# Six products of the second matmul taken to a second level inside PSUM, in the first two superblocks of an MLP block

## The chip, the cores and the metric

The kernel runs on one core of one Trainium2 chip. The metric is the device time in microseconds, the median of several runs. TensorE does the matmuls, VectorE sums, ScalarE copies and applies gelu, GpSimd casts, sums and issues DMAs, and SyncE issues most DMAs. "us" is a microsecond throughout.

## The reference

`x` is 8 x 1024 x 1024, `w1` 1024 x 4096 and `w2` 4096 x 1024, all float32. What is computed:

```
h = x @ w1
h = 0.5 * h * (1 + np.tanh(np.sqrt(2 / np.pi) * (h + 0.044715 * h ** 3)))
return (h @ w2).astype(np.float32)
```

## The kernel before

The 8192 rows of `x` are worked off in eight superblocks of 1024 rows. Each superblock has a first matmul (x by w1, with gelu, giving the four blocks g11, g12, g21, g22) and a second one (g by w2). Operands are float16, sums in PSUM float32.

**Seven products for eight.** Each matmul is cut into 2 x 2 blocks, and seven products of sums of blocks stand for the eight plain block products (Winograd's form of Strassen). The numbers 1, 2, 3, 4, 5, 6, 7 name the products; `W_SUM` says how the operand of the w side is summed for 5, 6, 7 and 4, and `S_SUM` how the other side is summed for 7, 6, 5 and 3. The same scheme can be applied again inside a product, with half the rows, half the columns and half the contraction: seven steps in place of eight, on matmuls of 256 columns. That is the second level. It needs inner sums of both operands.

**Which superblocks have it.** From superblock 2 on, both matmuls work on the second level (`Pair` and `Inner`, L659 and L984), with inner sums of w1 and w2 that lie in DRAM (`w1_d` with keys "s1" to "s5", `in_d`). Superblocks 0 and 1 build these sums and mostly work on one level: `matmul1` (L519) and `matmul2_made` (L807). In `matmul2_made` a product has four row groups q of 128 rows, each with 16 matmuls of 512 columns into one PSUM bank (`matmuls2`, L1057). The products run in the order 1, 2, 5, 6, 3, 7, 4.

**What sets the order.** Each engine's queue is in order. What VectorE does beside the products stands in the table `FILL` (L44): one row of jobs behind each (product, row group). `gmq` makes the g-side sums of product m; `wmq` makes the w2 sum m for one quarter of the contraction; `pmn` makes inner sum n of w2's product m and has GpSimd store it to `in_d`; `xm` sums blocks of the next superblock's x; `qm` sums w1 for the next superblock; `im` makes inner sums of x or of w1. In superblock 1 the w2 sums made by `make` (L839) are also stored to DRAM. `post` (L882) copies or adds a finished bank and issues the output store. SyncE's queue holds the loads of w2 (`bring`, L813, with float32 pieces that are cast in superblock 0), stores of the raw float16 blocks (`keep`, L832), the transposing loads of the next x, and loads of w1 (`MadeQuad`, L186), in the order of the program. SBUF tiles come from pools of fixed size: "u" has 26 buffers, "gc" 4, "tmp" 10; PSUM has 8 banks. A new tile waits until the last reader of the one it replaces has finished, which can be a DMA.

**Lines that the prediction's rows name.** L135 is the helper `tt` for VectorE sums, L159 `load_in_order` on SyncE, L162 the ScalarE copy, L165 the GpSimd cast, L195 loads of w1, L306 inner sums on GpSimd in later superblocks, L353 matmuls on zeros at the start, L485 one-level matmuls of the first matmul, L504 differences of g, L1012 second-level sums of g in later superblocks, L1059 one-level matmuls of the second matmul.

Of the kernel before, what the change touches and what calls it, by code (L numbers as in the profile page):

```python
# [39 lines left out]
def slots(table):  # L40
    return {(int(k[0]), int(k[1])): v.split() for k, v in (row.split(":") for row in table.split(";"))}


FILL = (  # L44
    slots("""10:g60 p15;11:g61 p16;12:g62 p17;13:g63
    ;20:g50 w50 w51;21:g51 w52;22:w53 g52;23:g53 p14
    ;50:w60 w61;51:w62 w63;52:g30 g31;53:g32 g33
    ;60:w70 w71;61:w72 w73;62:w40 w41;63:w42 w43
    ;73:x5;40:x7 x6;41:x3 q5;42:q6 q7 q4
    ;43:i2 i3 i1 i5""".replace("\n    ", "")),  # L50
    slots("""10:g60 w50;11:g61 w51;12:g62 w52;13:g63 w53
    ;20:g50 p55;21:g51 p56;22:g52 p57;23:g53 p54
    ;50:w60 w61;51:w62 w63;52:g30 g31;53:g32 g33
    ;60:p65 w70;61:p66 w71;62:p67 w72;63:p64 w73
    ;30:w40 w41;31:w42 w43;32:p75;33:p76
    ;70:p77 p74;71:x5 p45;72:x7 p46;73:x6 p47
    ;40:p44;41:x3;42:i2;43:i3""".replace("\n    ", "")),
)


# [11 lines left out]
def kernel(  # L72
# [113 lines left out]
    class MadeQuad:  # L186
# [52 lines left out]
            if self.store:  # L239
                nc.gpsimd.dma_start(out=w1_at(self.q, m), in_=halves(self.ops[m]))  # L240

        def inner_sums(self, m):
            t = self.ops[m].rearrange("p (h k c) (e n) -> p h k c e n", h=2, k=2, e=2)
            s = up.tile([P, 2, 4, 2, P], DT, name="u")

            def operand(b):
                if isinstance(b, int):
                    return s[:, :, list(S_SUM).index(b)]
                return t[:, :, int(b[1]) - 1, :, int(b[0]) - 1, :]

            for j, (u, op, v) in S_SUM.items():
                tt(operand(j), operand(u), operand(v), op, True)
            nc.gpsimd.dma_start(
                out=w1_at(self.q, f"s{m}"),
                in_=s.rearrange("p h j c n -> p h (j c n)"),
            )
# [55 lines left out]
    class XOps(dict):  # L312
# [5 lines left out]
            for m, b in S_TERM.items():  # L318
                self[m] = blocks[b]

        def make(self, m, cols=slice(None), pin=False):
            u, op, v = {5: ("21", ADD, "22"), 7: ("11", SUB, "21"), 6: ("22", SUB, 7), 3: ("12", SUB, 6)}[m]
            if m not in self:
                self[m] = self.blocks["21"] if m == 7 else unit(KH, HT)
            in0, in1 = (self[b] if isinstance(b, int) else self.blocks[b] for b in (u, v))
            tt(self[m][:, :, cols], in0[:, :, cols], in1[:, :, cols], op, pin)

        def make_inner(self, m):
# [187 lines left out]
            t = g[b][:, c:c + KH, :].rearrange("p c n -> p (c n)")  # L516
            yield t.rearrange("p (e n) -> p e n", e=2)

    def matmul1(xs, sb, quads, start=None):  # L519
        g = g_tiles()  # L520

        def gelu(b, c, src):
            gelu_into(g[b][:, c, :], src)
# [22 lines left out]
        for j in range(NI // 2):  # L546
# [62 lines left out]
            if end:  # L609
                six(0)  # L610
                gelu("11", cs[0], a[0])
                six(1)
                gelu("11", cs[1], a[1])
                for h in range(2):
                    five(h)
                for h in range(2):
                    seven(h)
                    gelu("22", cs[h], p5[h])
                    three(h)
                for h in range(2):  # L620
                    product(banks_a[h], source, xs, 4, cs[h], False)
                    gelu("21", cs[h], banks_a[h])
                for h in range(2):
                    add(t[h], banks_c[h])
                    gelu("12", cs[h], t[h])
            else:
                first = j == 0
                five(0)
                if not first:
                    gelu("11", cs[0], a[0])  # L630
                five(1)
                six(0)
                if not first:
                    gelu("11", cs[1], a[1])
                six(1)
                for h in range(2 if first else 0):
                    gelu("11", cs[h], a[h])
                three(0)
                three(1)
                seven(0)  # L640
                seven(1)
                for h in range(2):
                    gelu("22", cs[h], p5[h])
                for h in range(2):
                    add(t[h], banks_c[h])
                late = (source, cs, banks_a, t)
            for job in jobs[half:]:
                job()
            if sb == 1 and j < 2 * len(SPLIT_IN_M1):
                splits = split_in_m1(SPLIT_IN_M1[j // 2], j % 2)  # L650
            if sb == 1 and j > 4:
# [152 lines left out]
        rows = out2[r0:r0 + HT // 2, o0:o0 + OH].rearrange("(i p) n -> p i n", p=P)  # L804
        return nc.gpsimd.dma_start(out=rows, in_=src, **kw)  # L805

    def matmul2_made(sb, g, keep_w1, xb):  # L807


        raw = {b: [] for b in BLOCKS}  # L810
# [25 lines left out]

        over = {6: "11", 7: "12", 4: "21"}

        def make(m, q):  # L839
            if m not in sums:  # L840
                sums[m] = raw[over[m]] if m in over else [unit(2, HALF) for _ in range(NI // QC)]
            u, op, v = W_SUM[m]
            in0, in1 = (sums[b][q] if isinstance(b, int) else raw[b][q] for b in (u, v))
            tt(sums[m][q], in0, in1, op, True)
            if sb:
                n = 1 if q < 2 else 2
                nc.gpsimd.dma_start(out=w2_at(q, m)[:, :n], in_=sums[m][q][:, :n])

# [3 lines left out]
        def rows(t, q):  # L852
            return t[:, :, q * P:(q + 1) * P]

        s2, a, p5, t6, at = {}, {}, {}, {}, {}
        operands = {1: "11", 2: "12", 4: "22", 7: "21", 5: "11", 3: "12"}
        splits = {m: split_jobs(m, lambda m=m: pieces(m)) for m in (1, *SUMS)}

        def run(key):
            for job in FILL[sb].get(key, ()):  # L860
# [4 lines left out]
                elif kind == "g" and m == 5:  # L865
                    tt(rows(g["11"], n), s2[n], rows(g["11"], n), ADD, True)
                elif kind == "g":
                    tt(rows(g["12"], n), rows(g["12"], n), s2[n], SUB, True)
                elif kind == "w":
                    make(m, n)  # L870
                elif kind == "p":
                    splits[m][SUMS.index(n)]()
                elif kind == "x":
                    xs.make(m, pin=True)
                elif kind == "q":
                    quad.sum(m, pin=True)
                elif kind == "i" and sb:
                    xs.make_inner(m)
                elif kind == "i":
                    quad.inner_sums(m)  # L880

        def post(m, q, bank):  # L882
            if m in (1, 5, 6):
                t = {1: a, 5: p5, 6: t6}[m]
                t[q] = temp()
                act_copy(t[q], bank)
            elif m == 4:
                c = temp()
                act_copy(c, bank)
                store(sb, "21", q, c)  # L890
            else:
                t = {2: a, 3: t6, 7: p5}[m][q]
                tt(t, t, bank, ADD, True)
                at[q] = store(sb, {2: "11", 3: "12", 7: "22"}[m], q, t)

        bring("11", pool_copy, False)
        bring("21", pool_copy, False)
        bring("12", act_copy, True)
        keep("11")
        if sb:  # L900
            bring("22", None, False)
        banks = {"a": [], "b": [], "c": []}
        for m, name, first in (
            (1, "a", True), (2, "b", True), (5, "c", True), (6, "a", False),
            (3, "c", False), (7, "a", False), (4, "a", False),
        ):
            for q in range(NQ):
                if first:
                    banks[name].append(psum())
                bank = banks[name][q]  # L910
                matmuls2(bank, s2[q] if m == 6 else rows(g[operands[m]], q), pieces(m), first)
                post(m, q, bank)
                if (m, q) == (5, 0) and sb == 0:
                    xb = x_cast(sb + 1, nc.gpsimd.tensor_copy(out=pace, in_=p5[0][:, :2]))
                if (m, q) == ((5, 0) if sb else (6, NQ - 1)):
                    xs = XOps(x_transpose(xb, load_in_order))
                    keep("22")
                if (m, q) == (3, NQ - 1) and sb == 0:
                    quad = MadeQuad(0, False, True)
                if (m, q) == (4, 0) and sb:  # L920
                    quad = StoredHalf(0)
                if (m, q) == (1, NQ - 1) and sb == 0:
                    sums[5] = [unit(2, HALF) for _ in range(NI // QC)]
                    for t in sums[5]:
                        act_copy(t[:, 0, :1], warm)
                    bring("22", act_copy, True)
                    keep("21")
                    keep("12")
                run((m, q))
        return xs, [quad]  # L930

    def split_jobs(m, pieces):
        t = {}

        def operand(v, h):
            if isinstance(v, int):
# [13 lines left out]
    def split_in_m1(m, h):  # L950

        raw, t = [], {}
        for k in range(2):
            raw.append(gcp.tile([P, 2, HALF], DT, name="gc"))
            q = 2 * k + h
            nc.sync.dma_start(out=raw[k], in_=w2_at(q, m))

        def make(i, n):
            u, op, v = W_SUM[n]
# [197 lines left out]
    g_late = None  # L1157
    for sb in range(NSB):
        if sb < 2:
            g, nxt = matmul1(xs, sb, quads, first if sb == 0 else None)  # L1160
            xs, quads = matmul2_made(sb, g, None if sb else quads[-1].keep_raw, nxt)
            continue
        g, early, nxt = matmul1_late(xs, sb, quads, g_late or g_tiles())
        g_late, quads = matmul2(sb, g, early, nxt)
# [31 lines left out]
```

## Time and profile before

| | |
|---|---|
| median of 3 runs | 1466.68 us (1466.65 to 1466.9) |
| span of the profiled execution | 1464.9 us, so the median lies 1.8 us over it |
| instructions in the profile | 27508 |
| DMA | 462.15 MB, mean 315 GB/s |
| second matmul of superblock 0, first and second of superblock 1 | 96.69 us each, from 111.94, 208.63 and 305.32 us |

One execution was profiled. Times in rows count from the span's start. A group row has the source line, engine, operation, tiles and shapes, the number of instructions, then the busy time, the mean length of one in ns and the idle time ahead of them with what ended it. A matmul's length includes the time until its last result is written, so matmuls overlap and their lengths do not add up.

### The profile page before, as it was taken

The numbers are of one execution on the slowest core, as the hardware profiler recorded it, in microseconds if no ns is written. First come the engines' busy times: TensorE is split into PE (matmuls) and PEld (weight loads), VectorE is DVE, ScalarE is ACT, GpSimd is POOL, SyncE is SP. The second block draws the span as 40 slices with busy tenths as digits, with TensorE's granted clock in tenths as the row PEclk, the third lists the DMA queues.
The fourth block names the chain that finished last, engine by engine and source line by source line (L and its number), as shares of the span: only waits on it lengthen the run. The fifth ranks groups of instructions, "written<-read, shape, count | busy, mean of one in ns | idle before, by whom it ended". The sixth has DMA issues, their size and how long they took to land.

```text
span 1464.9 us, 27508 instructions
## 1 busy us (share of the span) xinstructions
PE 1456.8 (99%) x10383; PEld 1012.9 (69%) x10383; DVE 1166.0 (80%) x1940; ACT 600.7 (41%) x1226; POOL 443.6 (30%) x471
## 2 busy tenths in 40 slices
PE   8999999999999999999999999999999999999998
PEld 5444444444466788668876688767887678866787
DVE  6657459757677899879997799977998779887897
ACT  5665125631066411663126621366214652056410
POOL 1441123312347011560026501274103721136011
PEclk9999999999999999999999999999999999999999
DMA  9999899998998999979999899998999999996896
GB/s 330 342 349 392 229 342 360 385 300 230 353 323 215 360 276 366 375 207 373 307 369 338 203 373 326 359 305 248 350 346 347 297 280 313 352 367 215 310 302 206
DMA packets 207429, 462.15 MB, mean 315 GB/s; under 512 B 75840, under 2 KB 80960, under 8 KB 206400
## 3 DMA queue, kind: packets, MB, share of 16 engines
q1 hardware_dynamic: 179808, 364.96, 72.4%
q0 software_dynamic: 27488, 95.44, 21.9%
q8 instruction: 81, 1.33, 0.3%
q14 instruction: 52, 0.43, 0.1%
HBM read 361.76 MB, written 113.25 MB: 324 GB/s over the span
## 4 chain that ended last, share of the span: by engine, by line
PE 99%; DMA 1%; SPq 0%; DVE 0%; issue 0%; DVEq 0%
PE ps L1018 35%; PE ps L485 31%; PE ps L699 19%; PE ps L1059 13%; PE ps L418 1%; DMA gc<-in_w_dram 1%; SPq L159 0%; PE ps L395 0%; DVE u L223 0%; DVE u L135 0%; DVE u L406 0%; DVEq L135 0%
## 5 line engine op out<-in xcount | busy, mean ns | idle before, releaser
L485 PE MATMUL ps<-u 128*128 128x512 f16 x1808 | 423.5, 379 | 0.0
L135 DVE TENSOR_TENSOR tmp<-tmp,ps 128x512 f32<-128x512 f32 x498 | 280.3, 581 | 106.0 <-PE ps L485 44.6
L162 ACT COPY tmp<-ps 128x512 f32<-128x512 f32 (+1 forms) x398 | 209.4, 545 | 259.4 <-PE ps L1059 135.2
L135 DVE TENSOR_TENSOR ps<-tmp,ps 128x256 f32<-128x256 f32 x552 | 222.7, 425 | 102.9 <-PE ps L699 83.7
L1018 PE MATMUL ps<-u,gc 128*128 128x256 f16 x2688 | 300.3, 273 | 0.0
L485 PEld LDWEIGHTS <-u 128*128 128x128 f16 x1808 | 176.9, 98 | 170.2
L1018 PEld LDWEIGHTS <-gc 128*128 128x128 f16 x2688 | 263.0, 98 | 30.4
L699 PEld LDWEIGHTS <-u 128*128 128x128 f16 x2170 | 212.3, 98 | 67.9 <-issue 0.4
L498 ACT ACTIVATE g<-ps 128x512 f16<-128x512 f32 x326 | 192.9, 596 | 105.3 <-PE ps L699 64.9
L135 DVE TENSOR_TENSOR u<-u 128x2048 f16<-128x2048 f16 (+3 forms) x288 | 214.7, 787 | 23.6 <-DMA w_d<-u 10.9
L1018 PE MATMUL ps<-u,g 128*128 128x256 f16 x2016 | 227.9, 273 | 0.0
L162 ACT COPY u<-ps 128x512 f32<-128x512 f32 (+1 forms) x134 | 78.0, 587 | 354.9 <-PE ps L1018 348.0
L805 POOL DMA_DIRECT2D out_dram<-u x70 | 63.9, 936 | 498.2 <-DVE u L135 264.9
L1018 PEld LDWEIGHTS <-g 128*128 128x128 f16 x2016 | 197.2, 98 | 22.8
L699 PE MATMUL ps<-u 128*128 128x256 f16 x1298 | 193.6, 273 | 0.0
L135 DVE TENSOR_TENSOR u<-u,ps 128x512 f32<-128x512 f32 x216 | 147.7, 684 | 36.5 <-PE ps L1018 25.3
L1059 PE MATMUL ps<-u,g 128*128 128x512 f16 x768 | 166.4, 379 | 0.0
L498 ACT ACTIVATE g<-tmp 128x512 f16<-128x512 f32 x186 | 117.4, 633 | 99.0 <-DVE tmp L135 98.7
L306 POOL TENSOR_TENSOR u<-u 128x512 f16<-128x512 f16 x120 | 136.3, 1157 | 31.8 <-PE ps L699 22.4
L699 PE MATMUL ps<-gc,u 128*128 128x256 f16 x872 | 145.7, 273 | 0.0
L1059 PEld LDWEIGHTS <-g 128*128 128x128 f16 x768 | 75.1, 98 | 90.6
L1012 DVE TENSOR_TENSOR gc<-g,gc 128x2048 f16<-128x2048 f16 x84 | 102.4, 1220 | 3.1 <-PE ps L1018 3.1
(52 smaller groups left out, 854.8 us busy)
## 6 DMA issues: line engine op xcount, KB each, us to landing
u<-w_d SPq DMA_DIRECT2D x322, 512.0 KB, 9.1
u<-in_d SPq DMA_DIRECT2D x168, 512.0 KB, 7.9
out_dram<-u POOLq DMA_DIRECT2D x70, 512.0 KB, 10.8
gc<-in_w_dram SPq DMA_DIRECT2D x48, 512.0 KB, 6.0
g<-w_d SPq DMA_DIRECT2D x40, 512.0 KB, 12.0
w_d<-u POOLq DMA_DIRECT2D x36, 512.0 KB, 7.5
w_d<-u SPq DMA_DIRECT2D x32, 512.0 KB, 9.2
xb<-in_x_dram POOLq DMA_DIRECT2D x56, 256.0 KB, 6.8
```

Source lines behind the costliest of these rows:

```text
L135: i = nc.vector.tensor_tensor(out=out, in0=in0, in1=in1, op=op)
L162: tc.keep_in_program_order(nc.scalar.copy(out=out, in_=in_))
L306: nc.gpsimd.tensor_tensor(out=operand(j), in0=operand(u), in1=operand(v), op=op)
L418: tc.keep_in_program_order(nc.tensor.matmul(bank[:, cols], lhsT=w[:, k, :], rhs=self.xs.blocks[f"{a}{r}"][:, k, cols], start=r == 1 and k ...
L485: tc.keep_in_program_order(nc.tensor.matmul(bank, lhsT=w, rhs=x, start=first and k == 0, stop=k == n - 1, skip_group_check=not first,))
L498: gelu_last[0] = nc.scalar.activation(out=out, in_=src, func=GELU)
L699: tc.keep_in_program_order(nc.tensor.matmul(out, lhsT=w, rhs=x, start=first and k == 0, stop=k == 1, skip_group_check=not first,))
L805: return nc.gpsimd.dma_start(out=rows, in_=src, **kw)
L1012: tc.keep_in_program_order(engine.tensor_tensor(out=self.s[j], in0=in0, in1=in1, op=op))
L1018: tc.keep_in_program_order(nc.tensor.matmul(bank[:, i * OH // 2:(i + 1) * OH // 2], lhsT=t[:, c, i * P:(i + 1) * P], rhs=self.y[j][:, c, : ...
L1059: tc.keep_in_program_order(nc.tensor.matmul(pair(bank), lhsT=a[:, c, :], rhs=chunks(pieces[c // QC])[:, :, c % QC, :], start=(first and c ...
```

## The change

Second matmuls get a second level by a new class `Deep`: in superblock 0 products 7 and 4, in superblock 1 products 1, 2, 7 and 4. The seven steps run in the order 1, 5, 6, 2, 7, 3, 4, each for two halves i of 128 rows, and what they share is added up in PSUM. Step 1's result is copied by ScalarE into a second bank, step 5's into a temporary; after step 6 and after step 7 VectorE adds that temporary and the running half bank into another half bank, on which the next steps go on.

The job `sm` makes an inner sum of g for a deep product (a "gc" tile, or "u" for product 2), `Xm` is `xm` on GpSimd. The inner sums of w2's products 7 and 4 are made and stored in superblock 0 instead of 1, and so are the w2 sums 7 and 4 themselves. In superblock 0 they are operands of the deep products where they were made; in superblock 1 the deep products load theirs. The inner sums of w1's first quad (`i2 i3 i1 i5`) move from VectorE at the end of superblock 0 to GpSimd at the start of superblock 1, and the w2 sum 5 of superblock 1 moves to GpSimd ahead of product 1, where the four inner sums of g11 (the tail) are made on VectorE. Product 6's bank is now also copied to a tile "u" (v), on which products 7 and 4 are added.

The core of the diff:

```
+DEEP = ((7, 4), (1, 2, 7, 4))
+DEEP_STEPS = (1, 5, 6, 2, 7, 3, 4)
 FILL = (
...
-    ;73:x5;40:x7 x6;41:x3 q5;42:q6 q7 q4
-    ;43:i2 i3 i1 i5""".replace("\n    ", "")),
-    slots("""10:g60 w50;11:g61 w51;12:g62 w52;13:g63 w53
-    ;20:g50 p55;21:g51 p56;22:g52 p57;23:g53 p54
-    ;50:w60 w61;51:w62 w63;52:g30 g31;53:g32 g33
-    ;60:p65 w70;61:p66 w71;62:p67 w72;63:p64 w73
-    ;30:w40 w41;31:w42 w43;32:p75;33:p76
-    ;70:p77 p74;71:x5 p45;72:x7 p46;73:x6 p47
-    ;40:p44;41:x3;42:i2;43:i3""".replace("\n    ", "")),
+    ;30:p75 s75;31:p76 s77;32:s76 p77;33:s73 p74
+    ;70:p45 X5;71:p46 s45;72:s47;73:p47 X7;74:p44;75:s46 X6;76:s43
+    ;40:q5;41:q6 X3;42:q7;43:q4""".replace("\n    ", "")),
+    slots("""10:s25;11:s27;12:g60;13:s26 g61;14:s23;15:g62;16:g63
+    ;20:g50;21:g51;22:g52;23:g53;24:w60;25:w61
+    ;50:w62 w63;51:p55 p56;52:g30 g31;53:g32 g33
+    ;60:p57 p54;61:p65 p66;62:p67 p64;63:s75
+    ;30:s77;31:s76;32:s73
+    ;70:x5;71:x7;72:s45;73:x6;74:s47;75:x3;76:s46
+    ;40:s43;42:i2;43:i3""".replace("\n    ", "")),
 )
...
+            if sb == 1 and j == 0:
+                for m in (2, 3, 1, 5):
+                    quads[0].inner_sums(m, nc.gpsimd)
...
+        def step(self, j, i):
+            h, cols = {5: (1, right), 2: (0, left), 3: (0, right)}.get(j, (1, left))
+            bank = self.bank(2 * h + i)
+            t = self.x[S_TERM[j]] if j in S_TERM else self.s[j]
+            for c in range(NI // 2):
...
+            low = self.banks[2 + i]
+            if j == 1:
+                act_copy(self.bank(i)[:, left], low[:, left])
+            elif j == 5:
...
+                act_copy(self.copies[i], low[:, right])
+            elif j == 6:
+                tt(self.bank(i)[:, right], self.copies[i], low[:, left], ADD, True)
+            elif j == 7:
+                tt(low[:, right], self.copies[i], low[:, left], ADD, True)
...
-            if sb:
+            if sb != (m in DEEP[0]):
                 n = 1 if q < 2 else 2
                 nc.gpsimd.dma_start(out=w2_at(q, m)[:, :n], in_=sums[m][q][:, :n])
...
+            elif m == 7:
+                t = half_of(q)
+                tt(t, t, bank, ADD, True)
+                tt(p5[q], p5[q], t, ADD, True)
+                store(sb, "22", q, p5[q])
             elif m == 4:
-                c = temp()
-                act_copy(c, bank)
-                store(sb, "21", q, c)
+                t = half_of(q)
+                tt(t, t, bank, ADD, True)
+                store(sb, "21", q, t)
...
+        if sb:
+            deep[1].load((5, 6))
+            bring("12", None, True)
+            deep[1].load((7, 4))
+            for q in range(NI // QC):
+                make(5, q, nc.gpsimd)
+            bring("21", None, False)
...
+            if m in deep:
+                d = deep[m]
+                for n, j in enumerate(DEEP_STEPS):
+                    for i in range(2):
+                        d.step(j, i)
+                        if j in (3, 4):
+                            post(m, i if j == 3 else 2 + i, d.banks[i if j == 3 else 2 + i])
+                    events(m, n)
...
+            def tail(g):
+                early.append(Deep(1, g["11"], None))
+                for n in (5, 7, 6, 3):
+                    early[0].make(n, gcp)
```

A deep product's row in `FILL` is keyed by product and step position (70 to 76) instead of row group. Its jobs follow both halves of that step in the queues.

## The prediction

> **What bounds the kernel now.** I read the page's first part and its chain of what ended last, then the chain in order of time, then stretches and instructions around the change.
>
> ```profile
> PE 1456.8 (99%) x10383; PEld 1012.9 (69%) x10383; DVE 1166.0 (80%) x1940; ACT 600.7 (41%) x1226; POOL 443.6 (30%) x471
> PE 99%; DMA 1%; SPq 0%; DVE 0%; issue 0%; DVEq 0%
> ```
>
> The chain in time (start, length, what; x matmuls) names the stages:
>
> ```profile
> 111.94 96.69 PE ps L1059 x448
> 208.63 96.69 PE ps L485 x448
> 305.32 96.69 PE ps L1059 x448
> ```
>
> TensorE is never idle. These are the second matmul of superblock 0, the first and the second of superblock 1. A 512-column matmul costs 96.69/448 = 0.2158 us and a product (64 of them) 13.81. The chain's first stretch of the second level is 27.29 us for 250 matmuls of 256 columns, 0.1092 each. So anything that makes TensorE wait is added to the time, and only fewer columns shorten it.
>
> **What it removes.** Six products go from 64 matmuls of 512 to 7 steps of 16 matmuls of 256: 1.747 us a step, 12.23 a product, 1.58 less each, **9.5 us** for six (3.2 in superblock 0, 6.35 in superblock 1). The built order agrees: 6 x 48 = 288 matmuls more.
>
> **What it adds: waits inside a product.** Per half bank, ScalarE copies step 1 and step 5, VectorE adds after step 6 and step 7. The program's waits go by bank, so the half after next waits: only 8 matmuls, 0.87 us, lie between. A matmul's row lasts 0.379 though the next starts 0.216 later, so a result is there 0.16 late; then a copy of 0.38 or an add of 0.42. That makes some 0.6, which fits if the engine is free: 0 for the copies (ScalarE is 3% to 28% busy in these stages; 0.6 each, 14 us in all, if it were always late). VectorE isn't free. Its queue is in order and much stands in it before those adds.
>
> **VectorE in superblock 0.** Three answers for VectorE's instructions, then SyncE's issues with the landing (last column):
>
> ```profile
> 168.25 5.77 DVE L135 TENSOR_TENSOR u<-u 128x2048 f16<-128x2048 f16 x5 [0.35 <-DMA w_d<-u]
> 173.93 1.28 DVE L135 TENSOR_TENSOR tmp<-tmp,ps 128x512 f32<-128x512 f32 x2
> 202.07 1.23 DVE L135 TENSOR_TENSOR u<-u 128x2048 f16<-128x2048 f16 x1 [1.61 <-DMA u<-w_d]
> 206.27 2.36 DVE L135 TENSOR_TENSOR u<-u 128x2048 f16<-128x2048 f16 x2 [2.98 <-DMA u<-w_d]
> ```
>
> ```profile
> 187.93 3.78 SPq L159 DMA_DIRECT2D w_d<-u  x4
> w_d<-u SPq DMA_DIRECT2D x1, 512.0 KB, 3.4
> ```
>
> Five sums in 5.77 start 1.14 apart; adds of 512 and sums of 1024 start 0.6 apart (two end after 1.28). VectorE is done with the w2 sums at 173.93, as now (the jobs up to there are the same). Product 3's jobs then hold 4 adds, 8 half sums (p75 to p74) and 4 S sums: 2.4 + 4.8 + 4.56 = 11.8, to 185.7. Next is p45, whose output takes the buffer of the first piece of w2 block 22; that buffer's store is issued at 187.93, behind the transposes on SyncE, and lands 3.4 later, 191.3. Then p45 and p46 (2.4), s45 (1.14), and the add after step 6 (0.42): 195.3. TensorE, in product 7 since 181.0, wants it after three steps, 186.3: **9.0 us** idle. From there to the same add of product 4 stand 3 adds (1.5), p47 and p44 (2.4), 3 S sums (3.4), four pairs of output adds (5.2) and q5, q6 (2.3): 14.8 against 12.2 on TensorE, 2.6 more. (q6 waited for a load until 206.27; that is covered here, by 4 us, unless the 14 stores of 512 KB that move into this superblock delay it. 166 to 187 moved 149 GB/s against 365 earlier, so I cost them 0, with 3 us as the other end.) Superblock 0 alone: 9.0 + 2.6 - 3.2 = +8.4.
>
> **GpSimd's sums.** X5, X7, X6, X3, sixteen inner sums of w1 and four W5 sums move from VectorE to GpSimd. No row has a GpSimd sum beside a VectorE sum of two SBUF operands, but GpSimd casts stand there:
>
> ```profile
> 33.01 1.04 POOL L165 CAST u<-gc 128x1024 f16<-128x1024 f32 x1 [0.15 <-DMA gc<-in_w_dram]
> 112.92 1.27 POOL L165 CAST u<-gc 128x1024 f16<-128x1024 f32 x1 [0.45 <-DMA gc<-in_w_dram]
> ```
>
> ```profile
> 33.08 1.52 DVE L504 TENSOR_TENSOR g<-g,g 128x1024 f16<-128x1024 f16 x1
> 56.06 0.68 DVE L504 TENSOR_TENSOR g<-g,g 128x1024 f16<-128x1024 f16 x1
> 113.39 1.88 DVE L135 TENSOR_TENSOR gc<-g,g 128x2048 f16<-128x2048 f16 x1
> 116.40 1.21 DVE L135 TENSOR_TENSOR gc<-g,g 128x2048 f16<-128x2048 f16 x1
> ```
>
> The sum issued at 33.08 took 1.52, not 0.68, and ended 0.55 after the cast; the one at 113.39 took 0.67 more and ended 1.08 after the cast. The two ran one after the other. Adds with a PSUM operand kept 0.68 beside casts. GpSimd's sums by size:
>
> ```profile
> L306 POOL TENSOR_TENSOR u<-u 128x512 f16<-128x512 f16 x120 | 136.3, 1157 | 31.8 <-PE ps L699 22.4 <-DMA u<-w_d 6.5 <-PE ps L485 0.4
> L1012 POOL TENSOR_TENSOR gc<-g 128x2048 f16<-128x2048 f16 x6 | 24.4, 4074 | 0.0
> ```
>
> So the price lies between nothing and all of 4.07 (or 1.16) per sum that meets VectorE; below nothing too by 1.14 where VectorE isn't the late one. I take nearly all, since the casts were exclusive from begin to end. The Trainium skill (SBUF — State Buffer, "Who interferes with whom") says that VectorE with two SBUF inputs contends with a GpSimd instruction that reads SBUF and that the loser blocks for the full instruction; the casts agree, and no run here shows it for two-input sums. Sharing without loss would make the forecast the second rival below.
>
> - Superblock 0: X5 comes after p45's store is issued and stands before s45: +3.8, 12.8 idle instead of 9.0. X7 before p44 and X6 before the last output adds: 7.2 more, 9.8 instead of 2.6. X3 before q7: 2.0 at step 4. Behind them on GpSimd stand stores that no load waits for within 20 us, and X3 itself is done before the first matmul begins. Idle 24.6, less 3.2: **+21.4**.
> - First matmul of superblock 1:
>
> ```profile
> 209.00:234.00 25.00, 25.00 (x118) 11.30 (x116) 22.99 (x45) 15.17 (x29) 8.91 (x14) 1.00 1.01 381
> ```
>
>  Behind the stretch stand its length and the busy times of TensorE, weight loads, VectorE, ScalarE, GpSimd, then clock, DMA share and GB/s. VectorE has 23.0 of 25 us. The sixteen inner sums leave it: 16 x 0.37 (56 sums of 512 in 20.8) = 5.9. GpSimd's sixteen take 16 x 1.157 = 18.5 in the same stretch, between VectorE sums of two SBUF operands. 17.1 + 18.5 - 25 = **+10.6** (the other end 0).
> - Second matmul of superblock 1: between the last gelu and product 1's add after step 6, VectorE has four tail sums, a difference, s25, s27 (7.4), four adds (2.4) and that add: 10.2 against 10.7 on TensorE; the tail sums alone delay an add of the first matmul by 1.65. W5's four sums start 2.4 after that gelu and hold 4 x 4.07, of which about 14 falls on VectorE: 13.65 idle. In product 7 four pairs of adds, s47 and x3 stand before s46: 2.2 late. Product 2's adds find VectorE free. 13.65 + 2.2 - 6.35 = **+9.5**.
> - Loads: the deep operands of superblock 1 are issued 16 us or more of TensorE work ahead, against landings of 3.4 to 13.6: 0. SyncE's load of one of them stands behind W5's first sum, still 10 us early.
>
> **Sum.** 21.4 + 10.6 + 9.5 = 41.5 on a span of 1464.9: 1506.4. The median of 1466.68 lies 1.8 over that span; with the same around it **1508.2 us**.
>
> **Rivals.**
> - *Clock.* The start shows what a half clock costs:
>
> ```profile
> 1.19 3.17 PE L353 MATMUL ps<-idle 128*128 128x512 f16 x7 [1.19 <-DVE warm L1153]
> 5.67 0.59 PE L353 MATMUL ps<-idle 128*128 128x512 f16 x2
> ```
>
>  Seven matmuls start 0.427 apart, two later ones 0.216: 1.5 us lost per start from cold. Five idle stretches of the forecast last over 5 us. If each costs 1.5: 1508.2 + 7.5 = 1515.7. Against: gaps of 0.85 us at the start did no harm, and longer ones don't occur. The Trainium skill (TensorE: Matmul & The Clock Gate, "HAM oscillation") has the clock halved after idle gaps over about 3.4 us.
> - *GpSimd's sums cost VectorE nothing.* Then +8.4 in superblock 0, 0 in the first matmul, 1.65 + 2.2 - 6.35 = -2.5: 1472.6. Partial costs fall between this and the forecast. For: VectorE was never late beside GpSimd's 162 sums, but it had no such operands then.
> - *Faster.* VectorE's adds reach TensorE in time after all: p45's buffer is free before 185 and GpSimd costs nothing. Then 9.5 less: 1457.2. It decides at 0.87 us between step 6's half and its add. Against: the store is issued only at 187.93.
> - *Near no change.* As the second rival, with q jobs and stores 4 us better than I reckon: about 1468.
>
> **Numbers.** The forecast 0.58, clock 0.10, no or part cost of GpSimd 0.22, faster 0.06, near no change 0.04. The range reaches from below the second rival, 1470, to over the clock's, 1520, with 3 us for landings. 0.2% is 2.9 us, about what a measurement can tell: faster 0.06, same 0.04, slower 0.90.
>
> **What would show it.** In product 7 of superblock 0 TensorE waits 9 us or more on VectorE ahead of step 2, and the DMA of block 22 ends VectorE's wait at p45. VectorE's sums of 1.22 show rows of up to 5 beside GpSimd's X and W5 sums, and about twice 0.4 to 1.2 beside the inner sums. If those rows keep their length, the second rival holds; if p45 doesn't wait, the third. Matmul starts of 0.218 for 256 columns after a long wait would show the clock.

## The result and the profile after

The changed kernel takes **1536.99 us** (median of 4 runs, 1534.65 to 1537.71), the kernel before in the same session 1466.77 (1466.65 to 1466.9). The ratio is 1.0476, 95% interval 1.0461 to 1.0491. The forecast of 1508.2 had the direction right and the size wrong: 70 us were lost where 41.5 were foreseen, and 1520, the upper end of the range, was passed. The profiled execution has a span of 1535.5 us, 70.6 more than before.

The first part of the page of the changed kernel, and its shares of the chain that ended last:

```profile
PE 1461.0 (95%) x10671; PEld 1045.1 (68%) x10671; DVE 1228.8 (80%) x1972; ACT 608.2 (40%) x1250; POOL 499.7 (33%) x495
...
PE 90%; DVE 4%; DMA 2%; issue 2%; SPq 1%; ACT 0%; POOL 0%; DVEq 0%; ACTq 0%
```

TensorE has the 288 matmuls more that were counted, and is idle for 74.5 us of its span, against 8.1 before. Its share of the chain falls from 99% to 90%, and VectorE, DMA and SyncE's queue (SPq) come into it. What TensorE waited for (line, engine and line waited for, us in all, times, longest):

```profile
PE ps L868 <- DVE ps L138: 43.9, 3, 29.1
PE ps L495 <- DVE tmp L138: 10.2, 2, 5.5
PE ps L495 <- ACT tmp L165: 9.4, 2, 7.4
PE ps L868 <- DVE gc L138: 2.4, 2, 2.2
```

L868 is the matmul of `Deep.step`, L495 that of the first matmul. The third row names ScalarE, but its copies had no queue of their own; they stood behind a gelu that waited for VectorE's add.

From the starts of consecutive matmuls in the trace (the distance of two starts less the normal 0.2158 or 0.1092 us) one gets what was lost at each place. Distances of twice the normal one, behind a wait, are put down as half clock.

| us lost by TensorE | forecast | changed kernel |
|---|---|---|
| superblock 0, product 7, ahead of step 2 | 12.8 | 29.3 |
| superblock 0, product 4 | 11.8 | 8.2 |
| superblock 1, first matmul, sixteen inner sums | 10.6 | 14.6 (4.9, 7.5, 2.2) |
| superblock 1, from the tail to the end of the second matmul | 15.85 | 15.6 (5.6, 0.4, 7.2, 2.4) |
| half clock behind the waits | 0 | 10.9 |
| gain of six products | -9.5 | -9.5 |

The changed kernel's column sums to 69.1 of the 70.6. Three terms failed: the first, the third and the clock.

**The first wait.** VectorE in the changed kernel (start, length, tiles, number; in brackets the idle time before it and what ended it), at p45 and p46:

```profile
206.99 1.29 DVE L138 TENSOR_TENSOR u<-u 128x1024 f16<-128x1024 f16 x2 [18.87 <-DMA w_d<-u]
209.88 4.46 DVE L138 TENSOR_TENSOR u<-u 128x1024 f16<-128x1024 f16 x2 [1.60 <-DMA w_d<-u]
```

As foretold, p45 waits for the store of w2 block 22, but until 206.99 and not 191.3, and p46 waits for the second piece. SyncE's issues, first of the changed kernel, then of the one before:

```profile
168.13 35.55 SPq L162 DMA_TRANSPOSE u<-xb  x16
203.72 3.60 SPq L162 DMA_DIRECT2D w_d<-u  x4
```

```profile
166.22 21.67 SPq L159 DMA_TRANSPOSE u<-xb  x16
```

The sixteen transposes take 35.6 us to issue, not 21.7, and the store stands behind them. In that stretch (168 to 204) the DMA queue that GpSimd feeds, with the stores that the change moved here, takes 59.7% of the DMA engines' time, and 18.2% in the stretch of before that holds its transposes (166 to 188); a transpose lands after 7.3 us, not 3.2. These are the queue's rows (packets, MB, share) and the transposes' (us to landing), after and before:

```profile
q0 software_dynamic: 1792, 6.29, 59.7%
...
u<-xb SPq DMA_TRANSPOSE x16, 7.3
```

```profile
q0 software_dynamic: 386, 1.30, 18.2%
...
u<-xb SPq DMA_TRANSPOSE x16, 3.2
```

**GpSimd beside VectorE.** Both engines of the changed kernel at the last two W5 sums, VectorE first:

```profile
370.88 4.87 DVE L514 TENSOR_TENSOR g<-g,g 128x1024 f16<-128x1024 f16 x1 [2.18 <-ACT g L508]
375.67 6.84 DVE L138 TENSOR_TENSOR u<-g 128x2048 f16<-128x2048 f16 x2
```

```profile
371.12 4.07 POOL L927 TENSOR_TENSOR u<-u 128x2048 f16<-128x2048 f16 x1
...
376.11 4.17 POOL L927 TENSOR_TENSOR u<-u 128x2048 f16<-128x2048 f16 x1
```

The difference of g takes 4.87 us, alone 0.68: it ends 0.56 after GpSimd's sum. Two sums of g take 6.84, alone 2.35. In both pairs VectorE's row begins first, by 0.24 and 0.44 us, and VectorE is still the one that waits, so the starts of the rows don't tell which of the two goes first. VectorE's adds with a PSUM operand keep their 0.68 beside such sums. The Trainium skill (SBUF — State Buffer, "Who interferes with whom") has two-input VectorE sums contend with GpSimd's reads of SBUF and sums with one SBUF input not; here the trace agrees, in sums as it did in casts. Added up, VectorE's rows are 12.2 us longer than alone beside the X sums, 15.0 beside the inner sums and 12.4 beside W5.

### The profile page after: what moved, and what is told of

Same layout as the page of the kernel before. It is cut to its first block, busy times and chain, and to the rows that moved or that the text cites. A ratio compares the mean times of both kernels' runs of the same rounds, so it can differ in the third digit from the quotient of the medians.

```text
span 1535.5 us, 28262 instructions
## 1 busy us (share of the span) xinstructions
PE 1461.0 (95%) x10671; PEld 1045.1 (68%) x10671; DVE 1228.8 (80%) x1972; ACT 608.2 (40%) x1250; POOL 499.7 (33%) x495
## 4 chain that ended last, share of the span: by engine, by line
PE 90%; DVE 4%; DMA 2%; issue 2%; SPq 1%; ACT 0%; POOL 0%; DVEq 0%; ACTq 0%
PE ps L1161 33%; PE ps L495 27%; PE ps L714 18%; PE ps L1202 7%; PE ps L868 4%; DMA gc<-in_w_dram 1%; SPq L162 1%; DVE u L138 1%; DVE tmp L138 1%; DVE u L256 1%; PE ps L428 1%; DVE gc L138 1%; DVE g L514 0%; DMA w_d<-u 0%; DMA u<-w_d 0%
## 5 line engine op out<-in xcount | busy, mean ns | idle before, releaser
L495 PE MATMUL ps<-u 128*128 128x512 f16 x1808 | 429.8, 383 | 19.7 <-DVE tmp L138 10.2
L138 DVE TENSOR_TENSOR tmp<-tmp,ps 128x512 f32<-128x512 f32 x490 | 274.2, 578 | 79.7 <-PE ps L495 50.6
L138 DVE TENSOR_TENSOR ps<-tmp,ps 128x256 f32<-128x256 f32 x576 | 232.4, 425 | 105.9 <-PE ps L714 76.9
L495 PEld LDWEIGHTS <-u 128*128 128x128 f16 x1808 | 178.0, 98 | 194.6 <-issue 27.9
L165 ACT COPY u<-ps 128x512 f32<-128x512 f32 (+1 forms) x142 | 82.8, 587 | 354.9 <-PE ps L1161 347.9
L1161 PEld LDWEIGHTS <-g 128*128 128x128 f16 x2016 | 197.3, 98 | 22.8
L138 DVE TENSOR_TENSOR u<-u 128x512 f32<-128x512 f32 (+3 forms) x204 | 168.1, 858 | 34.7 <-DMA w_d<-u 20.5
L138 DVE TENSOR_TENSOR u<-u,ps 128x512 f32<-128x512 f32 x232 | 158.5, 684 | 37.7 <-PE ps L1161 28.5
L514 POOL TENSOR_TENSOR g<-g,g 128x1024 f16<-128x1024 f16 x36 | 76.6, 2127 | 93.7 <-ACT g L508 89.3
L1155 DVE TENSOR_TENSOR gc<-g 128x2048 f16<-128x2048 f16 x78 | 95.1, 1219 | 3.4 <-PE ps L1161 3.4
## 6 DMA issues: line engine op xcount, KB each, us to landing
g<-w_d SPq DMA_DIRECT2D x40, 512.0 KB, 11.8
```

The costliest lines, as they stand in the source:

```text
L138: i = nc.vector.tensor_tensor(out=out, in0=in0, in1=in1, op=op)
L165: tc.keep_in_program_order(nc.scalar.copy(out=out, in_=in_))
L495: tc.keep_in_program_order(nc.tensor.matmul(bank, lhsT=w, rhs=x, start=first and k == 0, stop=k == n - 1, skip_group_check=not first,))
L514: tc.keep_in_program_order(engine.tensor_tensor(out=g["21"][:, cs], in0=g["11"][:, cs], in1=g["21"][:, cs], op=SUB,))
L1155: tc.keep_in_program_order(engine.tensor_tensor(out=self.s[j], in0=in0, in1=in1, op=op))
L1161: tc.keep_in_program_order(nc.tensor.matmul(bank[:, i * OH // 2:(i + 1) * OH // 2], lhsT=t[:, c, i * P:(i + 1) * P], rhs=self.y[j][:, c, : ...
```

## The experiments

The theory after the result: (a) GpSimd's 24 sums hold VectorE and cost their length; (b) the stores that moved into superblock 0 slow the transposes and with them block 22's store; (c) what is left comes from VectorE's queue, in which too much stands ahead of an add that TensorE waits for. Rivals: GpSimd costs nothing and VectorE is just overfull; the transposes are slow for a reason of their own; the second level has waits that no order removes.

**sums_on_vector**: the changed kernel with all 24 sums on VectorE, at the same places.

```
-                    xs.make(m, engine=nc.gpsimd)
+                    xs.make(m, pin=True)
...
-                    quads[0].inner_sums(m, nc.gpsimd)
+                    quads[0].inner_sums(m)
...
-                make(5, q, nc.gpsimd)
+                make(5, q)
```

> All 24 sums that the change gave to GpSimd (4 X, 16 inner sums of w1, 4 W5) run on VectorE at the same places of its queue. Theory (a GpSimd sum and a VectorE sum of two SBUF operands run one after the other): in the changed kernel VectorE's rows are longer than alone by 12.2 us beside the X sums, 15.0 beside the inner sums and 12.4 beside W5, 39.6 in all; on VectorE the 24 sums cost 4 x 1.14 + 16 x 0.34 + 4 x 1.14 = 14.6; net 25 less idle on TensorE, and some 5 less of half clock: 1505 to 1515 us. The first wait of 29 us stays, shorter by 3 at most. No VectorE sum of 2048 elements over 1.3 us. Rival (VectorE is late because it has too much in its queue, and GpSimd's sums cost it nothing): 14.6 us more on VectorE, 1545 to 1552 us.

Measured: 1505.43 us, ratio 1.0264 (1.0240 to 1.0288), 31.6 less than the changed kernel. The theory's range just holds it, the rival is 40 us off. VectorE got 24 sums more, 14.6 us by their lengths alone, and the time fell. By place: 23.2 in product 7, 5.8 in product 4, 4.2 in the first matmul of superblock 1 (14.6), 7.8 from the tail on (15.6), half clock 7.4. The first wait is 6 us shorter, where 3 were expected at most: p45 starts 2.6 us earlier, at 204.36, and X5 no longer holds p46. The transposes still took 32.5 us, 3 less than in the changed kernel; why they took less isn't shown.

**stores_put_off**: the changed kernel with the moved stores on SyncE, behind block 22's store.

```
-                nc.gpsimd.dma_start(out=w2_at(q, m)[:, :n], in_=sums[m][q][:, :n])
+                if sb:
+                    nc.gpsimd.dma_start(out=w2_at(q, m)[:, :n], in_=sums[m][q][:, :n])
+                else:
+                    put_off.append((w2_at(q, m)[:, :n], sums[m][q][:, :n]))
...
                 keep("22")
+            if (m, q) == (3, 0) and sb == 0:
+                for to, t in put_off:
+                    load_in_order(to, t)
...
+            if sb == 0 and m in (7, 4):
+                load_in_order(in_d[m][:, SUMS.index(n)], t[n])
+            else:
+                nc.gpsimd.dma_start(out=in_d[m][:, SUMS.index(n)], in_=t[n])
```

> Of the change, only the stores that moved into superblock 0 (w2 sums 7 and 4, inner sums of products 7 and 4) go from GpSimd to SyncE's queue, behind the transposes and the store of w2 block 22. Theory (those stores share the DMA engines with the transposes and slow them): the 16 transposes are issued in 21 to 23 us as before (35.6 in the changed kernel), block 22's first piece is stored at 190 to 192, p45 starts at 194 to 196, TensorE's first wait is 14 to 16 us instead of 29.3, and the time is 1520 to 1525 us. Rival (the transposes are slow for another reason, such as the x they read landing 2 us later): 35 us again, 1534 to 1540.

Measured: 1526.48 us, ratio 1.0403 (1.0388 to 1.0419), 10.5 less than the changed kernel and 1.5 over the range given. SyncE's issues in this kernel:

```profile
168.21 21.21 SPq L162 DMA_TRANSPOSE u<-xb  x16
189.46 11.74 SPq L162 DMA_DIRECT2D w_d<-u  x12
```

The transposes are back at 21.2 us with a start at 168.2 as in the changed kernel, so the later landing of x isn't the cause; the stores are. The edit takes them off GpSimd's queue and off this stretch at once, so which of the two counts isn't told apart. The first wait is 18.0, not 14 to 16: with no stores between them on GpSimd, X7 follows X5 at once and both hold p46's two halves. VectorE, then GpSimd, in this kernel:

```profile
195.52 7.88 DVE L138 TENSOR_TENSOR u<-u 128x1024 f16<-128x1024 f16 x2 [1.58 <-DMA w_d<-u]
```

```profile
194.35 8.50 POOL L333 TENSOR_TENSOR u<-u 128x2048 f16<-128x2048 f16 x2 [9.00 <-DMA w_d<-u]
```

**put_off_on_vector**: both edits.

> Both edits: the 24 sums on VectorE and the stores put off to SyncE's queue. If both theories hold their savings add up (25 + 5 and 15): 1488 to 1497 us, with a first wait of 10 to 13 us and the rest in the places where VectorE's queue alone is too long. If GpSimd's sums cost nothing: 1530 or more.

Measured: 1496.91 us, ratio 1.0202 (1.0185 to 1.0219), in the range given. The first wait is 11.6. Savings add up to 40.1 of the 42.1 that the two gave alone.

**keep_first_put_off_on_vector**: the same, and block 22 is stored ahead of the transposes.

```
+                if sb == 0:
+                    keep("22")
                 xs = XOps(x_transpose(xb, load_in_order))
-                keep("22")
+                if sb:
+                    keep("22")
```

> As put_off_on_vector (all 24 sums on VectorE, moved stores behind on SyncE), and the store of w2 block 22 goes ahead of the transposes on SyncE. Theory: the rest of the first wait (11.6 us of TensorE) is the wait of p45 and p46 for that store; with it gone VectorE is through p45, p46, s45 and X5 at 193.5 instead of 198 against 186.9 on TensorE, so the wait is 6 to 8 us and the time 1490 to 1494 us. Rival (VectorE's queue alone makes the wait): 11 us again, 1496 to 1498.

Measured: 1495.56 us, ratio 1.0193 (1.0179 to 1.0207). The first wait falls from 11.6 to 3.8, below what was expected, so 7.8 of it were that store. But the time hardly moves, 1.4 us and above the range: in product 4 the wait grows from 7.1 to 12.2. VectorE there, at q5:

```profile
211.65 1.23 DVE L138 TENSOR_TENSOR u<-u 128x2048 f16<-128x2048 f16 x1 [5.55 <-DMA u<-w_d]
```

q5 waits for w1 of the next superblock, whose loads stand behind the put-off stores on SyncE. The gain came back as another wait on the same queue.

**one_level_put_off_on_vector**: as put_off_on_vector, but superblock 0's products 7 and 4 on one level; their w2 sums and inner sums are still made and stored there.

```
-DEEP = ((7, 4), (1, 2, 7, 4))
+DEEP = ((), (1, 2, 7, 4))
...
```

> As the last one, but superblock 0's products 7 and 4 stay on one level (their w2 sums and inner sums are still made and stored there), so that only superblock 1 has deep products. Theory: without an add that TensorE waits for inside a product, the wait of VectorE for block 22's store falls on no matmul; the four deep products of superblock 1 give 6.35 back, and the adds of product 1 come late by VectorE's queue (4 tail sums, a difference, 4 W5 sums, s25, s27: 14.4 us against 10.7 on TensorE): 1462 to 1470 us. Rival (VectorE's work moved into superblock 0 delays the banks of product 7 and the first matmul of superblock 1): 1475 to 1490.

Measured: 1491.38 us, ratio 1.0164 (1.0149 to 1.0179): the theory's range is missed by 21 us, and the rival's by 1. TensorE loses 5.6 us at the start of the first matmul of superblock 1, where it waits for a load of w1 behind the put-off stores, 10.2 further on, and 7.8 from the tail on. VectorE ahead of the 10.2:

```profile
233.54 1.22 DVE L138 TENSOR_TENSOR u<-u 128x2048 f16<-128x2048 f16 x1 [5.39 <-DMA u<-w_d]
...
236.51 7.42 DVE L256 TENSOR_TENSOR u<-u 128x512 f16<-128x512 f16 x20
```

It waits 5.4 us for the next piece of w1, late for the same reason, and then has twenty inner sums ahead of the add that TensorE needs. So the stores put off to SyncE cost even where no product of superblock 0 is deep: they delay the loads behind them.

**before_inner_on_gpsimd**: the kernel before with one part of the change, the sixteen inner sums of w1 on GpSimd.

```
-    ;43:i2 i3 i1 i5
...
+            if sb == 1 and j == 0:
+                for m in (2, 3, 1, 5):
+                    quads[0].inner_sums(m, nc.gpsimd)
```

> The kernel before with one part of the change alone: the 16 inner sums of w1's first quad move from VectorE at the end of superblock 0 to GpSimd at the start of the first matmul of superblock 1. Theory (one after the other): in the 25 us from 209 us VectorE has 17.1 us of its own left and loses 15 (as in the changed kernel's rows) to 18.5 (16 x 1.157) to GpSimd, so TensorE waits 7 to 10.6 us there, and 2 to 4 more for a half clock: 1474 to 1481 us. Rival (GpSimd's sums cost VectorE nothing, the stage's waits in the changed kernel come from what superblock 0 left late): 1466 to 1467.5.

Measured: 1484.27 us, ratio 1.0118 (1.0103 to 1.0134); the rival falls, and the theory was too low by 3 us or more. TensorE waits 14.4 us (4.9, 7.9, 1.6) and loses 2.7 to the clock. Two stretches of this kernel (behind each its length, then the busy times of TensorE, weight loads, VectorE, ScalarE and GpSimd, the clock, DMA share and GB/s):

```profile
209.00:225.80 16.80, 16.80 (x79) 7.60 (x78) 8.62 (x14) 9.74 (x19) 2.48 (x4) 1.00 0.72 283
225.80:251.50 25.70, 16.71 (x69) 7.09 (x68) 25.56 (x22) 7.38 (x14) 24.79 (x22) 0.93 0.49 176
```

GpSimd's sums run from 225.8 to 251.5, and VectorE is busy all that time. Its 8.2 us of spare time lie in the stretch before, where they are of no use.

**superblock1_products_1_2**: superblock 0, the sums of w2, their stores and the inner sums of w1 as before; deep are products 1 and 2 of superblock 1 alone, and the tail makes only two of its four sums.

```
-DEEP = ((7, 4), (1, 2, 7, 4))
+DEEP = ((), (1, 2))
...
+    slots("""10:s16;11:s13;12:s25 g60;13:s27 w50;14:s26 g61 w51;15:s23 g62 w52;16:g63 w53
+    ;20:g50;21:g51;22:g52;23:g53;24:p55;25:p56;26:p57
...
-                for n in (5, 7, 6, 3):
+                for n in (5, 7):
                     early[0].make(n, gcp)
```

> Only products 1 and 2 of superblock 1 are deep; superblock 0, w2's sums and all stores are as before, no sum goes to GpSimd; only two of the four sums of g11 are made in the tail, the others behind product 1's first step, and W5 is made beside product 1 and 2. Theory: the change's losses all come from moved sums and stores and from a too long VectorE queue ahead of an add that TensorE waits for; with these avoided two products give 2 x 1.58 = 3.2 us: 1463 to 1465 us. Rival (a second level in these products has a wait of its own, as the 3.1 us at product 1's add that stayed with all sums on VectorE): 1466 to 1470.

Measured: 1472.91 us, ratio 1.0039 (1.0026 to 1.0052): worse than both expected. What TensorE waited for:

```profile
PE ps L864 <- DVE ps L137: 5.1, 2, 4.9
```

Product 1 has no long wait any more, so the 3.1 us seen there were the queue. The 4.9 (with 2.3 of half clock) are at product 2's add after step 6: VectorE reached it at 328.0, with ten sums of 1.14 between product 1's last adds and this one.

**superblock1_products_1_2_4**: the same with product 4 of superblock 1 deep too, on sums made in place.

> As the last one with product 4 of superblock 1 deep too, on w2 sums made in place. Theory: 3 x 1.58 = 4.7 us less, if VectorE, with 4 sums and 4 adds more in products 7 and 4 (12.9 and 13.2 us of 13.8 and 12.2), stays in time: 1462 to 1465. Rival: product 4's adds or the next superblock's x sums come late by 1 to 5 us: 1464 to 1470.

Measured: 1470.76 us, ratio 1.0033 (1.0019 to 1.0046), again above both ranges. The same 5.0 at product 2, and 0.6 at product 4.

**products_1_2_sums_later** and **products_1_2_4_sums_later**: sums that aren't needed yet go behind product 2's add.

```
+    slots("""10:s16;11:s13;12:s25;13:s27;14:s26 g60;15:s23 w50;16:w51
+    ;20:w52;22:g50 w53;23:g61;24:g51;25:g62;26:g52
+    ;50:g63 w60;51:g53 w61;52:w62 g30;53:w63 g31
...
```

> As superblock1_products_1_2, but what stood on VectorE ahead of product 2's add after step 6 and isn't needed by then (three of the g sums for 6, two W5 sums, g51) goes behind it, and the inner sums of products 5, 6 and 7 move on by up to a product. Theory: the 5.0 us of TensorE at that add (and 2.3 of half clock behind it) came from VectorE's queue being 4.2 us too long; without it the two products give 3.2 us less some 0.8 of short waits: 1463.5 to 1465.5 us. Rival (the moved sums come late at products 5, 6 or 4 instead): 1467 to 1473.

> The same with product 4 of superblock 1 deep too. Theory: another 1.58 less 0.6 of a wait seen at product 4: 1462 to 1465 us. Rival (VectorE has 14.2 us of work in product 3 and some 15 in product 4, for 13.8 and 12.2 on TensorE, and comes late for product 4 or for the next superblock): 1466 to 1472.

Measured: 1465.43 us, ratio 0.9990 (0.9981 to 0.9999), and 1464.4 us, ratio 0.9984 (0.9975 to 0.9993). Both lie in the theory's ranges. The long wait is gone. What is left are 0.4 us in the first, and 0.4 and 1.9 in the second. In the first, TensorE's last matmul ends 2.4 us earlier than in the kernel before (1458.2 for 1460.6), but the span is only 1.1 shorter; what is lost behind the last matmul stays open.

**products_1_2_4_evened**: the inner sums are moved forward into the 3 us that VectorE sat idle in product 6.

```
+    ;60:g32 g33 p56;61:p57 p54 w70;62:w71 p65;63:w72 w73 p66 p67
+    ;30:p64 w40;31:w41 w42;32:w43 p75;33:p76 p77
+    ;70:p45 s45;71:p46 s47;72:s46 p47;73:x5
+    ;40:s43;41:p44;42:x7 p74;43:x6;44:x3;45:i2;46:i3
```

> As products_1_2_4_sums_later, with the inner sums moved a row or more earlier into the 3 us in which VectorE had nothing to do at the end of product 6, and one x sum moved behind product 4's second add. Theory: the one wait of 1.9 us left at product 4's first add goes, since VectorE then reaches it some 2 us earlier: 1462.3 to 1463.3 us. Rival (the x sums or inner sums that move come late for the next superblock): 1464.4 or more.

Measured: **1463.31 us** (1463.11 to 1463.9), ratio 0.9975 (0.9965 to 0.9985): faster than the kernel before by 3.6 us, of 4.7 that three products can give, at the slow end of the theory's range. Its page:

```profile
PE 1452.6 (99%) x10527; PEld 1025.2 (70%) x10527; DVE 1186.7 (81%) x1968; ACT 604.1 (41%) x1238; POOL 442.7 (30%) x471
```

TensorE is busy for 99% of the span again, with 144 matmuls more than before.

## Why the prediction was wrong in size

- **What the products give** was right: 1.58 us each. In the last version three of them bring 3.6 us with 0.4 and 0.9 of waits left.
- **The wait of p45** was right in its place and its cause: VectorE, behind block 22's store, ahead of step 2 of product 7. Its size failed at one term: the stores moved into superblock 0 were costed at 0, with 3 us as the other end, because the stretch moved only 149 GB/s. (They are 16, four of them of 256 KB, as many bytes as the 14 of 512 KB that the working counts.) They slowed the transposes by 13.9 us (35.6 for 21.7); with 1.9 of a later start these are the 15.7 by which p45 starts after the forecast 191.3. stores_put_off shows it (21.2). The low mean rate before the change said little about what the transposes bear. The row that it was read from, and that of the 365 GB/s, have the DMA engines' share just ahead of the rate:

```profile
105.00:126.00 21.00, 21.00 (x99) 9.47 (x97) 12.16 (x15) 12.72 (x18) 7.78 (x9) 1.00 0.98 365
166.00:187.00 21.00, 21.00 (x99) 9.51 (x98) 10.84 (x12) 0.59 (x1) 2.76 (x5) 1.00 0.68 149
```

  At 149 GB/s the engines were busy for 68% of the time, so some 6.7 of the 21 us were free. An estimate from these rows: the eleven stores that came into the stretch hold 5.0 MB, 13.6 us at 365 GB/s, so some 7 us had to be added, where 0 was put.
- **GpSimd's sums against VectorE's** was right, and right to take nearly whole: VectorE's rows grew by 39.6 of the 51.1 us that the 24 sums have alone, and sums_on_vector gained 31.6 us. For W5 and what follows it the sum fitted (15.85, measured 15.6), though 5.6 of it fell on an add of the first matmul, where 1.65 were foreseen; in product 4 it was high (11.8, measured 8.2), since X7 met VectorE only in part.
- **The first matmul of superblock 1** was too small: 10.6, measured 14.6, and 14.4 in before_inner_on_gpsimd. The step credited VectorE's spare time of a 25 us stretch against sums that run later. The waits are about what VectorE's rows gained in length beside these sums (15.0): the whole gain in length was paid.
- **The clock** was a rival with a tenth of the chance and 7.5 us; it happened, with 10.9. The argument against it, gaps of 0.85 us at the start, came from gaps far shorter than those forecast. The forecast counted five waits over 5 us (its terms name four: 12.8, 9.8, 10.6, 13.65) and should have taken the price that it had worked out. The half clock didn't come behind every wait; the last section shows what decided. Clock in the changed kernel behind the first wait, and behind a wait of 2.4 us (length, TensorE's busy time, clock, DMA):

```profile
216.30:219.80 3.50, 3.50 (x19) 0.53 1.01 377
...
463.90:467.00 3.10, 3.10 (x31) 1.00 0.88 315
```

Together: 16.5 of the first wait, 4.0 in the first matmul and 10.9 of clock, less 3.6 and 0.25 where it was high, are 27.5 of the 29 us by which the forecast was low. A part of the errors cancelled. One thing stays open: whether the transposes suffer from the traffic itself or from GpSimd's queue beside SyncE's; no run separates them.

## What to carry to other kernels

Before a sum is moved to GpSimd, look at what VectorE does at that moment: with two SBUF operands on both sides most of GpSimd's length is paid (39.6 of 51.1 us here), at the worst place in the queue, and spare time elsewhere in the stage does not help. A store that is moved is a change to every queue it shares engines with: look at the transfers beside it, above all at those that another engine's buffer waits for. When an add becomes something that TensorE waits for, write the in-order queue out up to that add, and put behind it all that isn't needed yet; here this alone turned a loss into a small gain.

## What the runs showed of the hardware

- Sixteen DMA transposes were issued in 21 to 24 us where only a few stores ran beside them, and in 32 to 36 beside nine to eleven more stores of 256 and 512 KB from GpSimd, single ones in up to 5.1.
- VectorE sums with two SBUF operands and GpSimd sums alternate instruction by instruction: two half sums of 0.68 took 7.88 beside two GpSimd sums of 4.04 and 4.38, and a GpSimd inner sum of 1.16 stretched to 2.14 beside VectorE.
- The half clock lasted 2 to 5.5 us and cost 1.2 to 2.8 a time. It came behind all waits of 3.1 us and more. Of seven waits of 2.4 it came behind two (in stores_put_off and keep_first_put_off_on_vector), and behind none of up to 2.2. The Trainium skill (TensorE: Matmul & The Clock Gate, "HAM oscillation") speaks of gaps over about 3.4; the waits of 2.4 and 3.1 lie under it, so the measurement decides.
- What divides the waits of 2.4 is where they fall. The clock's records change only on a grid of 3.41 us, whose start differs from run to run. In the nine runs with half clock, every one of the 33 grid steps at full clock in which TensorE was idle for 2.06 us or more was followed by a step at half clock, and none of the 21 with 1.0 to 1.99 us was. The wait of 2.4 (2.23 idle) in keep_first_put_off_on_vector lies inside one step, the one in the changed kernel in two. For each, the step with the most idle time and the next one, first keep_first_put_off_on_vector, then the changed kernel (length, TensorE's busy time, clock, DMA share and GB/s):

```profile
416.88:420.29 3.41, 1.18 (x12) 1.00 1.02 417
420.29:423.70 3.41, 3.41 (x19) 0.50 1.01 387
```

```profile
461.93:465.34 3.41, 1.77 (x17) 1.00 0.95 286
465.34:468.75 3.41, 3.41 (x34) 1.00 0.97 338
```
